# Latent attention: slots and rotary tables laid out anew, and another order of the filling work between the heads

## The chip, the cores and the metric

The kernel runs on one core of one Trainium2 chip. The metric is the device time of one execution in microseconds (us). Three runs of the kernel before took 1540.17, 1544.18 and 1545.57 us; the median is 1544.18 us. The profile is of one more execution.

The engines in this text are PE (TensorE: matrix products and transposes), DVE (VectorE: additions, products, reductions on tiles), ACT (ScalarE: casts, exponentials, square roots), POOL (GpSimd) and SP (SyncE), which here mostly issue transfers (DMAs).

## The reference

The model is a trunk of two layers on 528 positions: 16 learned meta tokens and 512 frames, each a vector of 1024 floats. Layer 0 mixes with retention, layer 1 with latent attention; each is followed by a gated feed-forward network (FFN) of hidden width 2816. Only layer 1's attention is touched by the change:

```
kv_a  = rmsnorm(h) @ w_kv_a                   # latent of 512, rotary key of 64
k, v  = rmsnorm(kv_a[:512]) @ w_kv_b          # 8 heads: 128 key, 128 value channels
cq    = rmsnorm(rmsnorm(h) @ w_q_a)           # 768
q     = cq @ w_q_b                            # 8 heads: 128 plain, 64 rotary channels
q_rot = [q1 * cos - q2 * sin, q1 * sin + q2 * cos]
for each block of 128 queries:
    sc = (q . k + q_rot . k_rot) * 192 ** -0.5, masked to earlier chunks of 64
    o  = softmax(sc) @ v
h = h + concat(o) @ w_o
h = h + (silu(n @ w1) * (n @ w3)) @ w2        # n = rmsnorm(h), the FFN behind it
```

## The kernel before

**Arithmetic.** Every product of two float32 tiles is made of three matmuls on tiles of a shorter float format: each operand is split into a high part `hi` and a low part `lo` (`split`, L320: ACT casts `hi`, DVE subtracts for `lo`), and `mm` (L358 and L360) adds hi x hi, hi x lo and lo x hi. The weights come by `weights` (L345): SP loads `raw`, ACT casts `whi`, DVE subtracts `wlo`, in a ring of three buffers each.

**Memory.** `slot()` (L279) takes a tile of 128 x 528 from the pool `sp` (45 slots in this stage) or from `yp`, eight slots at the right end of the memory. `temp()` takes one of the short-lived tiles `t`, `wide()` one of `e`. `acc` and `r` are constants of one slot's size, used for the norms; between the norm ahead of the attention and the FFN's norm both are idle. PSUM, where PE writes, holds four tiles `ps` of 1024 columns (`pp`); every product, every score block, every set of transposes takes one and gives it back when its last reader is done. A request for a tile waits until the one that has to be used again is free.

**The stage.** `mla` (L973) first makes the latent `ckv` and the query latent `cq`, and loads the rotary tables: `ktr` for the key, two tiles `qtr` for the queries. Then come two kinds of work, written out one behind the other in program order, which each engine follows.

*The heads* (loop from L1113). The 512 queries are four blocks. For head `n`, `scores(i)` makes block `i`'s scores with five products per stretch (L113), the maximum on DVE, the exponential on ACT (L124, tile `t`), and DVE scales the result (L126). `weights(i)` transposes that on PE (L139, L140) and splits it into `e` tiles; the 16 meta rows go to `meta_p` (L331). `values()` is twelve products (L156) and one with the meta rows (L157); its result is split into two slots and joins the list `att`. The loop runs a head behind: block 3's transposes and the values of head n-1 stand between the first scores of head n.

*The filling work.* `Filler` (L65) holds a dictionary of generators. `step()` takes the next step of the first one in the dictionary; `FILL[n]` (L56) says how many steps go into each of five gaps of head `n`. `until(name)` runs the first entries to their ends until `name` is gone; the loop calls `until(f"q{n}")` before head `n`. The generators are

- `query(n)`: one step, head n's queries (18 matmuls of L360 and a split).
- `rotary(g)`: the rotary channels of four heads; two products, then `rotate_queries` (L1171), where DVE multiplies with the tables and ACT and POOL's DMAs copy 32-row pieces into four heads' tiles (L1187).
- `keys_values(pr)`: seven steps for a pair of heads: two key products (L358, 24 rows of two matmuls), four value tiles and, as the fifth, the meta tokens' (`mla_values`, L1156; matmuls at L620).
- `project(pairs, g)`: four steps, each a product of six matmuls with half of the output weights and the addition to the residual `h[m]`. While the pair's two heads are not both in `att`, a step of it is empty (L1076).

**The tail** (L1133 to L1141). Behind head 7's last values, `until("p2")` runs what is left of the first half of pair 2's projection, `project([3], 0)` makes the first half of pair 3's, and `project([2, 3], 1)` makes the second halves of both in one sum. Each of its steps with pair 3 also calls `prep_ffn` (L479): ACT scales `h[m]` to an FFN input, `square_add` (L387) adds its squares to `acc` on DVE, and for every second `m` `operands` (L758) makes seven sums and splits them to the tile `xp`. Then the FFN begins (L910): its weights come as `raw`, some of them summed (`raw <- raw`), split to `whi` and `wlo`, and products go to PSUM tiles `a` and `b` (L827). `start` (L933) sums the squares and takes the root (L930).

Of the kernel before, what the change touches and what calls it, by code (L numbers as in the profile page):

```python
# [12 lines left out]
F32R = mybir.dt.float32r  # L13
# [6 lines left out]
P = 128  # L20
D = 1024
KD = D // P
SEQ = 512
META = 16
T = SEQ + META
# [17 lines left out]
RING = 3  # L43
EW = 4 * HT
RET_SLOTS = 45
MLA_SLOTS = 45

PARTS = (3, 3, 2, 3)

# [10 lines left out]
def drain(steps):  # L60
    for _ in steps:
        pass
# [26 lines left out]
class Head:  # L89
# [57 lines left out]
    def values(self):  # L147
        k, nc = self.k, self.nc
        po = k.ps()
        c = slice(self.vi * P, (self.vi + 1) * P)  # L150
        for j in range(4):
            vh, vl = (u[:, c] for u in self.v[j])
            q0 = min(j, 2) * P
            ph, pl = (z[j // 2][:, j % 2, q0:] for z in (self.ph, self.pl))
            for t, (x, y) in enumerate(((vh, ph), (vh, pl), (vl, ph))):
                nc.tensor.matmul(po[:, q0:SEQ], x, y, start=j == 0 and t == 0, stop=False)  # L156
        nc.tensor.matmul(po[:, :SEQ], self.v[4][:, c], self.pm[:, :SEQ], start=False, stop=True)  # L157
        pool = k.yp if self.n >= 2 else None
# [89 lines left out]
class Kernel:  # L248
# [724 lines left out]
    def mla(self):  # L973
        nc, a = self.nc, self.a
# [7 lines left out]
        r = self.r  # L982
        ktr = self.slot()
        nc.gpsimd.dma_start(out=ktr, in_=a["ktrig"])
        qtr = [self.slot(), self.slot()]
        for i in range(2):
            nc.gpsimd.dma_start(out=qtr[i][:, :SEQ], in_=a["qtrig"][:, i])
        self.ident = self.const([P, P], name="ident", src=a["ident"])
        self.ma = self.const([P, P], BF16, name="ma")
        nc.vector.memset(self.ma, 0.0)  # L990
# [40 lines left out]
            nc.gpsimd.dma_start(out=z[ROPE:P], in_=z[0:ROPE])  # L1031
        for _ in steps:
            next(norm, None)
        drain(norm)
        self.meta_tiles(ckv)

# [4 lines left out]
        def keys_values(pr):  # L1041

            kn = []
            whi, wlo = self.weights(a["w_kbk"][pr])
            for i in range(2):
                ps = self.ps()
                for k in range(4):
                    c = slice((i * 4 + k) * P, (i * 4 + k + 1) * P)
                    self.mm(ps, (whi[:, c], wlo[:, c]), ckv[k], k == 0, k == 3, True)
                hi, lo = (self.slot(F32R, None if pr else self.yp) for _ in range(2))  # L1050
# [46 lines left out]
        for i, _ in enumerate(norm):  # L1097
            if i % 2:
# [4 lines left out]
        drain(query(1))  # L1103


        order = {"q2": query(2), "q3": query(3), "r1": rotary(1), "q5": query(5), "p0": project([0], 0),
                 "p0b": project([0], 1), "kv2": keys_values(2), "q4": query(4), "kv3": keys_values(3), "q6": query(6),
                 "q7": query(7), "p1": project([1], 0), "p1b": project([1], 1), "p2": project([2], 0)}
        filler = Filler(order)
        prev = None  # L1110
        for n in range(MH):
# [21 lines left out]
        prev.weights(3)  # L1133
        filler.step()
        att.append(prev.values())
        filler.until("p2")
# [4 lines left out]
        drain(project([2, 3], 1))  # L1141

    def normed(self, raw, acc, name, n, full, out):
        w = T if full else SEQ
# [11 lines left out]
    def mla_values(self, pr, ckv, out):  # L1156

        w = self.weights(self.a["w_kbv"][pr])
        w = [[u[:, k * 256 : (k + 1) * 256] for u in w] for k in range(4)]
        pool = None if pr else self.yp  # L1160
        v = [(self.slot(F32R, pool), self.slot(F32R, pool)) for _ in range(2)]
        for j in range(5):
            if j < 4:
                c = (j % 2) * 256
                out.append([u[:, c : c + 256] for u in v[j // 2]])
            else:
                out.append(self.meta_v[pr // 2][:, pr % 2 * 256 : (pr % 2 + 1) * 256])
            self.token_rows(ckv, self.xm, w, j, out[j])
            yield

    def rotate_queries(self, got, tr, heads):  # L1171

        p1, p2 = got
        c, s = (z[:, :SEQ] for z in tr)
        parts = []
        for u, w, op in ((c, s, ALU.subtract), (s, c, ALU.add)):
            m1, m2 = self.slot()[:, :SEQ], self.slot()[:, :SEQ]
            self.tt(m1, p1, u, ALU.mult)
            self.tt(m2, p2, w, ALU.mult)
            parts.append((m1, m2, op))  # L1180
        for half, (m1, m2, op) in enumerate(parts):
            self.tt(m1, m1, m2, op)
            hi, lo = (self.slot(F32R)[:, :SEQ] for _ in range(2))
# [101 lines left out]
```

## Time and profile before

| | |
|---|---|
| runs | 1540.17, 1544.18, 1545.57 us (median 1544.18) |
| profiled execution | 1546.48 us; its span 1544.5 us |
| PE busy | 1442.9 us, 93% of the span |
| DVE busy | 1170.7 us, 76% |
| ACT busy | 768.0 us, 50% |
| POOL busy | 152.3 us, 10% |
| chain that ended last | PE 31%, DVE 8%, ACT 3%, DMA 1% of the span |
| DMA | 183.87 MB, mean 119 GB/s |

The span runs from the first to the last instruction in the trace; the execution's own time is 2.0 us longer. Times below are counted from the span's start. PE is the busy engine of the whole, but its share is a mean over stages. The latent attention lies between about 840 and 1165 us of the span; its heads run from about 960 to 1130 us, its tail from there on. In a timeline, a row is a run of like instructions: its start, its length, engine, line, operation, tiles, shape, count, and in brackets the idle time of the engine ahead of it with what ended that.

### The profile page before, as it was taken

The numbers are of one execution on the slowest core, as the hardware profiler recorded it, in microseconds if no ns is written. First come the engines' busy times: TensorE is split into PE (matmuls) and PEld (weight loads), VectorE is DVE, ScalarE is ACT, GpSimd is POOL, SyncE is SP. The second block draws the span as 40 slices with busy tenths as digits, with TensorE's granted clock in tenths as the row PEclk, the third lists the DMA queues.
The fourth block names the chain that finished last, engine by engine and source line by source line (L and its number), as shares of the span: only waits on it lengthen the run. The fifth ranks groups of instructions, "written<-read, shape, count | busy, mean of one in ns | idle before, by whom it ended". The sixth has DMA issues, their size and how long they took to land. (4 is left out here: it accounts for less than half of the span.)

```text
span 1544.5 us, 27868 instructions
## 1 busy us (share of the span) xinstructions
PE 1442.9 (93%) x10988; PEld 1388.2 (90%) x10988; DVE 1170.7 (76%) x1901; ACT 768.0 (50%) x1365; POOL 152.3 (10%) x196
## 2 busy tenths in 40 slices
PE   8999999999996999999988999899978999999984
PEld 8999999999996999989988988688858999989974
DVE  7675485484597998978988677676786988979886
ACT  5452342352465555545556446545465555545542
POOL 2000000000000111111121001000001111111120
PEclk9999999999998999999999999899988999999997
DMA  6222222122143667677656223201225776677562
GB/s 216 79 69 83 79 71 95 55 83 83 56 109 89 171 159 196 162 171 174 164 134 167 82 83 100 75 28 66 55 62 137 175 180 167 161 185 180 140 151 70
DMA packets 84803, 183.87 MB, mean 119 GB/s; under 512 B 9777, under 2 KB 30385, under 8 KB 84673
## 3 DMA queue, kind: packets, MB, share of 16 engines
q1 hardware_dynamic: 60336, 141.13, 29.3%
q0 software_dynamic: 24336, 40.98, 15.6%
q8 instruction: 86, 1.41, 0.4%
q14 instruction: 45, 0.36, 0.1%
HBM read 178.65 MB, written 2.10 MB: 117 GB/s over the span
## 5 line engine op out<-in xcount | busy, mean ns | idle before, releaser
L827 PE MATMUL b<-xp,whi 128*128 128x264 f32 (+1 forms) x2640 | 493.7, 287 | 23.2 <-ACT t L883 10.7
L322 ACT CAST whi<-raw 128x1024 fp32r<-128x1024 f32 (+5 forms) x428 | 364.2, 855 | 299.8 <-PE ps L358 152.1
L318 DVE TENSOR_TENSOR wlo<-raw,whi 128x1024 fp32r<-128x1024 f32 (+5 forms) x428 | 413.8, 977 | 61.2 <-ACT whi L322 59.1
L827 PEld LDWEIGHTS b<-xp,whi 128*128 128x128 f32 x2640 | 414.9, 192 | 26.7 <-ACT t L883 11.9
L827 PE MATMUL b<-xp,wlo 128*128 128x264 f32 (+1 forms) x1320 | 376.6, 285 | 0.0
L358 PE MATMUL ps<-s,whi 128*128 128x264 f32 x1824 | 303.2, 288 | 11.1 <-ACT whi L322 6.5
L358 PEld LDWEIGHTS ps<-s,whi 128*128 128x128 f32 x1824 | 256.9, 191 | 13.4 <-ACT whi L322 6.5
L827 PEld LDWEIGHTS b<-xp,wlo 128*128 128x128 f32 x1320 | 253.0, 192 | 0.0
L827 PE MATMUL a<-xp,whi 128*128 128x264 f32 (+1 forms) x1056 | 204.4, 289 | 5.0 <-ACT whi L322 5.0
L358 PE MATMUL ps<-s,wlo 128*128 128x264 f32 x912 | 187.2, 287 | 0.0
L827 PE MATMUL a<-xp,wlo 128*128 128x264 f32 (+1 forms) x528 | 156.3, 296 | 22.7 <-DVE wlo L318 21.9
L827 PEld LDWEIGHTS a<-xp,whi 128*128 128x128 f32 x1056 | 168.2, 194 | 5.7 <-ACT whi L322 5.6
L358 PEld LDWEIGHTS ps<-s,wlo 128*128 128x128 f32 x912 | 143.3, 191 | 0.1
L799 POOL DMA_DIRECT2D raw<-w x76 | 65.9, 867 | 774.5 <-DMA raw<-w 368.5
L827 PEld LDWEIGHTS a<-xp,wlo 128*128 128x128 f32 x528 | 102.9, 195 | 29.0 <-DVE wlo L318 28.7
L360 PE MATMUL ps<-s,whi 128*128 128x512 f32 x368 | 120.0, 407 | 4.3 <-ACT t L124 3.5
L620 PE MATMUL ps<-whi,s 128*128 128x256 f32 x640 | 115.4, 281 | 0.0
L318 DVE TENSOR_TENSOR s<-ps,s 128x256 fp32r<-128x256 f32 (+4 forms) x96 | 51.7, 557 | 71.2 <-ACT s L322 49.1
L620 PEld LDWEIGHTS ps<-whi,s 128*128 128x128 f32 x640 | 98.9, 188 | 0.2
L802 POOL DMA_DIRECT2D raw<-w x76 | 65.6, 863 | 250.2 <-DMA raw<-w 102.0
L620 PE MATMUL ps<-wlo,s 128*128 128x256 f32 x320 | 89.5, 280 | 0.0
L360 PEld LDWEIGHTS ps<-s,whi 128*128 128x128 f32 x368 | 68.8, 193 | 20.6 <-ACT t L124 4.1
(158 smaller groups left out, 1811.0 us busy)
## 6 DMA issues: line engine op xcount, KB each, us to landing
raw<-w SPq DMA_DIRECT2D x140, 256.0 KB, 3.8
raw<-w SPq DMA_DIRECT2D x44, 512.0 KB, 4.9
raw<-w POOLq DMA_DIRECT2D x88, 256.0 KB, 5.2
raw<-w SPq DMA_DIRECT2D x72, 192.0 KB, 3.1
raw<-w SPq DMA_DIRECT2D x24, 384.0 KB, 3.6
raw<-w POOLq DMA_DIRECT2D x48, 192.0 KB, 4.3
raw<-w_v SPq DMA_DIRECT2D x16, 512.0 KB, 3.8
raw<-w_g SPq DMA_DIRECT2D x16, 512.0 KB, 3.5
```

What stands on the lines that cost most here:

```text
L318: self.nc.vector.tensor_tensor(out=out, in0=a, in1=b, op=op)
L322: self.nc.scalar.copy(out=hi, in_=src)
L358: mm(ps[:, h * 512 : h * 512 + HT], w[p], x[q][:, h * HT : (h + 1) * HT], start=s, stop=e)
L360: mm(ps[:, :SEQ], w[p], x[q], start=s, stop=e)
L620: mm(ps[:, :256], x[k][p][:, c], w[k][q], start=k == 0 and i == 0, stop=k == last and i == 2)
L799: nc.gpsimd.dma_start(out=q.r1[:, 1], in_=q.part(3), accum_op=ALU.add)
L802: nc.gpsimd.dma_start(out=q.r3[:, 0], in_=q.part(0), accum_op=ALU.add)
L827: nc.tensor.matmul(bank, wt[u][:, cs], xp[:, p, v, :w], start=first and k == 0 and i == 0, stop=False, skip_group_check=True)
```

## The change

It has three parts, all in layer 1's attention.

- **Slots.** The two rotary tables of the queries go to `acc` and `r` and are loaded later, behind the query latent and behind the DMAs that copy the rotary key. In `rotate_queries` one of two products and the high part become temporaries, and the last subtraction or addition is written in the first loop. `sp` has 47 slots. `yp` serves the keys and values of pairs 0 and 2 (before: pair 0 alone) and the outputs of heads 6 and 7 (before: of heads 2 to 7).
- **Order.** In the filling table `q4` and `kv2` now stand ahead of pair 0's projection, `q5` behind it.
- **The second half of pair 2's projection** is an entry of its own (`p2b`), ended before the tail; the tail's last call has pair 3 alone.

```
--- before.py
+++ after.py
@@ -43,7 +43,7 @@
 RING = 3
 EW = 4 * HT
 RET_SLOTS = 45
-MLA_SLOTS = 45
+MLA_SLOTS = 47
 
 PARTS = (3, 3, 2, 3)
 
@@ -155,7 +155,7 @@
             for t, (x, y) in enumerate(((vh, ph), (vh, pl), (vl, ph))):
                 nc.tensor.matmul(po[:, q0:SEQ], x, y, start=j == 0 and t == 0, stop=False)
         nc.tensor.matmul(po[:, :SEQ], self.v[4][:, c], self.pm[:, :SEQ], start=False, stop=True)
-        pool = k.yp if self.n >= 2 else None
+        pool = k.yp if self.n >= 6 else None
         hi, lo = k.slot(F32R, pool), k.slot(F32R, pool)
         k.split(hi[:, :SEQ], lo[:, :SEQ], po[:, :SEQ])
         return hi, lo
@@ -982,9 +982,7 @@
         r = self.r
         ktr = self.slot()
         nc.gpsimd.dma_start(out=ktr, in_=a["ktrig"])
-        qtr = [self.slot(), self.slot()]
-        for i in range(2):
-            nc.gpsimd.dma_start(out=qtr[i][:, :SEQ], in_=a["qtrig"][:, i])
+        qtr = [self.acc, r]
         self.ident = self.const([P, P], name="ident", src=a["ident"])
         self.ma = self.const([P, P], BF16, name="ma")
         nc.vector.memset(self.ma, 0.0)
@@ -1031,6 +1029,8 @@
             nc.gpsimd.dma_start(out=z[ROPE:P], in_=z[0:ROPE])
         for _ in steps:
             next(norm, None)
+        for i in range(2):
+            nc.gpsimd.dma_start(out=qtr[i][:, :SEQ], in_=a["qtrig"][:, i])
         drain(norm)
         self.meta_tiles(ckv)
 
@@ -1047,7 +1047,7 @@
                 for k in range(4):
                     c = slice((i * 4 + k) * P, (i * 4 + k + 1) * P)
                     self.mm(ps, (whi[:, c], wlo[:, c]), ckv[k], k == 0, k == 3, True)
-                hi, lo = (self.slot(F32R, None if pr else self.yp) for _ in range(2))
+                hi, lo = (self.slot(F32R, None if pr % 2 else self.yp) for _ in range(2))
                 self.split(self.two(hi), self.two(lo), self.halves(ps))
                 kn.append((hi, lo))
                 yield
@@ -1103,9 +1103,7 @@
         drain(query(1))
 
 
-        order = {"q2": query(2), "q3": query(3), "r1": rotary(1), "q5": query(5), "p0": project([0], 0),
...
+        order = {"q2": query(2), "q3": query(3), "r1": rotary(1), "q4": query(4), "kv2": keys_values(2), "p0": project([0], 0), "p0b": project([0], 1), "q5": query(5), "q6": query(6), "kv3": keys_values(3), "q7": query(7), "p1": project([1], 0), "p1b": project([1], 1), "p2": project([2], 0), "p2b": project([2], 1)}
         filler = Filler(order)
         prev = None
         for n in range(MH):
@@ -1133,12 +1131,12 @@
         prev.weights(3)
         filler.step()
         att.append(prev.values())
-        filler.until("p2")
+        filler.until("p2b")
         self.shut("sp", "mm")
         self.wx = self.pool("wx")
         self.xp = self.pool("xp", bufs=4)
         drain(project([3], 0))
-        drain(project([2, 3], 1))
+        drain(project([3], 1))
 
     def normed(self, raw, acc, name, n, full, out):
         w = T if full else SEQ
@@ -1157,7 +1155,7 @@
 
         w = self.weights(self.a["w_kbv"][pr])
         w = [[u[:, k * 256 : (k + 1) * 256] for u in w] for k in range(4)]
-        pool = None if pr else self.yp
+        pool = None if pr % 2 else self.yp
         v = [(self.slot(F32R, pool), self.slot(F32R, pool)) for _ in range(2)]
         for j in range(5):
             if j < 4:
@@ -1174,13 +1172,14 @@
         c, s = (z[:, :SEQ] for z in tr)
         parts = []
         for u, w, op in ((c, s, ALU.subtract), (s, c, ALU.add)):
-            m1, m2 = self.slot()[:, :SEQ], self.slot()[:, :SEQ]
+            m1, m2 = self.slot()[:, :SEQ], self.temp()[:, :SEQ]
             self.tt(m1, p1, u, ALU.mult)
             self.tt(m2, p2, w, ALU.mult)
-            parts.append((m1, m2, op))
-        for half, (m1, m2, op) in enumerate(parts):
             self.tt(m1, m1, m2, op)
-            hi, lo = (self.slot(F32R)[:, :SEQ] for _ in range(2))
+            parts.append(m1)
+        for half, m1 in enumerate(parts):
+            hi = self.tp.tile([P, T], F32R, tag="tmp", name=self.name("t"))[:, :SEQ]
+            lo = self.slot(F32R)[:, :SEQ]
             self.split(hi, lo, m1)
             for j in range(4):
                 to, of = half * 32, slice(32 * j, 32 * j + 32)
```

How the instructions move on three engines, at the places that the prediction speaks of:

PE, at the end of head 1: behind the scores of its fourth block stand the transposes of its second and third, then (`L113`, 128x256) head 2's first scores. `ps` are PSUM tiles, `t` the scaled softmax blocks. Before:

```order
L115 MATMUL ps_11300<-mb,ma 128x64
L139 MATMUL ps_11319<-ident,t_11218 128x128 x2
L140 MATMUL ps_11319<-ident,t_11218 16x128
L139 MATMUL ps_11328<-ident,t_11279 128x128 x3
L140 MATMUL ps_11328<-ident,t_11279 16x128
L113 MATMUL ps_11340<-s_10658,s_10995 128x256
```

and of the change, where the tile `whi`/`wlo` holds the key weights of pair 2:

```order
L358 MATMUL ps_11361<-s_10406,wlo_11254 128x264 x2
L358 MATMUL ps_11361<-s_10447,whi_11253 128x264 x2
L358 MATMUL ps_11361<-s_10448,whi_11253 128x264 x2
L358 MATMUL ps_11361<-s_10447,wlo_11254 128x264 x2
L139 MATMUL ps_11390<-ident,t_11312 128x128 x3
L140 MATMUL ps_11390<-ident,t_11312 16x128
L113 MATMUL ps_11402<-s_10656,s_10993 128x256
L113 MATMUL ps_11402<-s_10657,s_10993 128x256
```

The transposes of the second block (`x2`) and of the third (`x3`) stood next to each other before; now the second key product of pair 2 (24 rows, of which the last four are seen) stands between them. The first key product stands in the gap ahead of head 0's values, where before had an empty step.

ACT, around the first exponential of head 1 (`L124`). `s` in the casts of `L322` is the high part of a rotary half, the casts of `L1187` (of the change `L1186`) copy its rows to the four heads, `ps` of 128x128 is a transposed block of head 0. Before:

```order
L322 CAST s_11147<-s_11138 128x512
L322 CAST e_11043<-ps_11159 128x128
L1187 CAST s_11134<-s_11138 32x512
L1187 CAST s_11135<-s_11138 32x512
L1187 CAST s_11136<-s_11138 32x512
L329 CAST meta_p_1251_9782<-ps_11159 16x128
L124 ACTIVATE t_11178,mx_11179<-ps_11171,mx_11179 128x144
```

and of the change:

```order
L322 CAST t_11146<-s_11136 128x512
L1186 CAST s_11132<-s_11136 32x512
L1186 CAST s_11133<-s_11136 32x512
L1186 CAST s_11134<-s_11136 32x512
L1186 CAST s_11135<-s_11136 32x512
L322 CAST e_11041<-ps_11158 128x128
L124 ACTIVATE t_11177,mx_11178<-ps_11170,mx_11178 128x144
```

Before, three of the four copies of the first half stand ahead of the exponential; now all four do, and the first of them stand ahead of the cast of head 0's block.

DVE, at the end of the attention. `h_64` to `h_71` are the eight residual tiles, the first to be added to in the tail is `h_64`; `s` is the low part of head 7's output. Before:

```order
L318 TENSOR_TENSOR meta_p_1252_9783<-ps_12677,meta_p_1252_9783 16x128
L318 TENSOR_TENSOR raw_1830_12922<-raw_12924 128x512
L318 TENSOR_TENSOR s_12705<-ps_12690,s_12704 128x512
L318 TENSOR_TENSOR h_64<-ps_12722,h_64 128x512
L318 TENSOR_TENSOR h_65<-ps_12733,h_65 128x512
L318 TENSOR_TENSOR e_12746<-e_12730 128x256
L318 TENSOR_TENSOR h_66<-ps_12757,h_66 128x512
L318 TENSOR_TENSOR e_12746<-e_12730,e_12746 128x256
```

and of the change, from the first addition behind head 7's last transposed block on:

```order
L318 TENSOR_TENSOR h_68<-ps_12712,h_68 128x512
L318 TENSOR_TENSOR s_12703<-ps_12688,s_12702 128x512
L318 TENSOR_TENSOR h_69<-ps_12720,h_69 128x512
L318 TENSOR_TENSOR h_70<-ps_12728,h_70 128x512
L318 TENSOR_TENSOR h_71<-ps_12736,h_71 128x512
L318 TENSOR_TENSOR raw_1832_12928<-raw_12930 128x512
L318 TENSOR_TENSOR wlo_12944<-raw_12926,whi_12943 128x1024
L318 TENSOR_TENSOR h_64<-ps_12758,h_64 128x512
L318 TENSOR_TENSOR h_65<-ps_12769,h_65 128x512
```

Four additions of pair 2's second half (`h_68` to `h_71`) now stand ahead of the tail's first one, and so does the low part `wlo` of an FFN weight, which before stood behind the tail's operands.

## Rows read from the trace of the kernel before

**Rows 1.** `Windows` of core 0: busy us and instructions per engine, then clock, DMA.

```profile
960.00:1020.00 60.00, 50.69 (x260) 41.56 (x259) 36.88 (x96) 31.46 (x81) 3.89 (x8) 0.91 0.23 66
1020.00:1056.00 36.00, 34.42 (x235) 30.89 (x234) 24.37 (x61) 18.02 (x48) 0.00 (x0) 1.00 0.20 67
1056.00:1113.00 57.00, 55.55 (x354) 48.63 (x353) 42.13 (x111) 30.50 (x84) 0.93 (x1) 1.00 0.19 55
```

**Rows 2.** Timeline of PE, heads 0 to 2: start, length, line, tiles, count, idle.

```profile
980.92 0.84 PE L113 MATMUL ps<-s,s 128*128 128x256 f32 x5
...
986.56 1.22 PE L360 MATMUL ps<-s,whi 128*128 128x512 f32 x2 [2.92 <-ACT t L124]
...
998.60 1.48 PE L113 MATMUL ps<-s,s 128*128 128x264 f32 x10 [1.55 <-ACT t L124]
...
1003.13 0.90 PE L139 MATMUL ps<-ident,t 128*128 128x128 f32 x3 [2.65 <-ACT t L124]
...
1003.90 1.42 PE L113 MATMUL ps<-s,s 128*128 128x256 f32 x5
...
1007.27 0.90 PE L113 MATMUL ps<-s,s 128*128 128x272 f32 x5 [0.91 <-ACT meta_p L331]
```

**Rows 3.** Timeline of ACT in head 1, same columns.

```profile
983.96 1.89 ACT L1187 CAST s<-s 32x512 fp32r<-32x512 f32 x3
...
986.04 0.38 ACT L124 ACTIVATE t<-ps,mx 128x144 f32<-128x144 f32 x1
```

**Rows 4.** Groups by line and shape, 930 to 1131 us: busy us, mean ns.

```profile
L322 ACT CAST s<-ps 128x256 fp32r<-128x256 f32 x12 | 4.4, 373 | 4.4 <-PE ps L620 4.2
```

**Rows 5.** Timeline of DVE, last use of `r` and first rotary products.

```profile
916.38 0.69 DVE L318 TENSOR_TENSOR s<-ps,r 128x512 f32<-128x512 f32 x1 [2.29 <-PE ps L360]
...
945.75 1.89 DVE L318 TENSOR_TENSOR s<-ps,s 128x512 f32<-128x512 f32 x3 [2.52 <-PE ps L360]
```

**Rows 6.** Timeline of PE, end of head 7 and last projections.

```profile
1124.88 0.63 PE L139 MATMUL ps<-ident,t 128*128 128x128 f32 x4 [2.84 <-DVE t L126]
...
1126.08 0.79 PE L156 MATMUL ps<-e,s 128*128 128x512 f32 x1 [0.46 <-ACT e L322]
...
1127.53 2.51 PE L156 MATMUL ps<-e,s 128*128 128x512 f32 x11
...
1130.11 0.40 PE L360 MATMUL ps<-s,wlo 128*128 128x512 f32 x1
...
1130.81 0.39 PE L360 MATMUL ps<-s,wlo 128*128 128x512 f32 x1
```

**Rows 7.** Timeline of PE, first products of layer 1's FFN.

```profile
1151.79 0.63 PE L827 MATMUL a<-xp,whi 128*128 128x256 f32 x2
1155.85 0.58 PE L827 MATMUL a<-xp,wlo 128*128 128x256 f32 x1 [3.44 <-DVE wlo L318]
1156.23 0.63 PE L827 MATMUL a<-xp,whi 128*128 128x256 f32 x2
```

**Rows 8.** Timeline of DVE, from the last values to the first FFN product.

```profile
1130.31 0.69 DVE L318 TENSOR_TENSOR raw<-raw 128x512 f32<-128x512 f32 x1 [2.35 <-PE ps L157]
1130.93 0.69 DVE L318 TENSOR_TENSOR s<-ps,s 128x512 fp32r<-128x512 f32 x1
1132.44 1.29 DVE L318 TENSOR_TENSOR h<-ps,h 128x512 f32<-128x512 f32 x2 [0.82 <-PE ps L360]
...
1152.64 1.02 DVE L318 TENSOR_TENSOR xp<-e,xp 128x512 fp32r<-128x512 f32 x2
...
1154.58 2.35 DVE L318 TENSOR_TENSOR wlo<-raw,whi 128x1024 fp32r<-128x1024 f32 x2
```

**Rows 9.** Timeline of ACT in the same stretch.

```profile
1154.69 1.04 ACT L322 CAST xp<-e 128x1024 fp32r<-128x1024 f32 x1 [1.96 <-DVE e L318]
1158.39 0.36 ACT L860 COPY b<-a 128x256 f32<-128x256 f32 x1 [2.65 <-PE a L827]
...
1161.34 0.47 ACT L930 ACTIVATE r<-a,eps_rms 128x256 f32<-128x256 f32 x1 [0.33 <-PE a L929]
```

More of the change, by code (lines that the diff above doesn't have):

```diff
@@ L157, in values @@
         nc.tensor.matmul(po[:, :SEQ], self.v[4][:, c], self.pm[:, :SEQ], start=False, stop=True)
-        pool = k.yp if self.n >= 2 else None
+        pool = k.yp if self.n >= 6 else None
         hi, lo = k.slot(F32R, pool), k.slot(F32R, pool)
@@ L984, in mla @@
         nc.gpsimd.dma_start(out=ktr, in_=a["ktrig"])
-        qtr = [self.slot(), self.slot()]
-        for i in range(2):
-            nc.gpsimd.dma_start(out=qtr[i][:, :SEQ], in_=a["qtrig"][:, i])
+        qtr = [self.acc, r]
         self.ident = self.const([P, P], name="ident", src=a["ident"])
@@ L1033, in mla @@
             next(norm, None)
+        for i in range(2):
+            nc.gpsimd.dma_start(out=qtr[i][:, :SEQ], in_=a["qtrig"][:, i])
         drain(norm)
@@ L1049, in keys_values @@
                     self.mm(ps, (whi[:, c], wlo[:, c]), ckv[k], k == 0, k == 3, True)
-                hi, lo = (self.slot(F32R, None if pr else self.yp) for _ in range(2))
+                hi, lo = (self.slot(F32R, None if pr % 2 else self.yp) for _ in range(2))
                 self.split(self.two(hi), self.two(lo), self.halves(ps))
@@ L1103, in mla @@
         drain(query(1))
-        order = {"q2": query(2), "q3": query(3), "r1": rotary(1), "q5": query(5), "p0": project([0], 0),
-                 "p0b": project([0], 1), "kv2": keys_values(2), "q4": query(4), "kv3": keys_values(3), "q6": query(6),
-                 "q7": query(7), "p1": project([1], 0), "p1b": project([1], 1), "p2": project([2], 0)}
+        order = {"q2": query(2), "q3": query(3), "r1": rotary(1), "q4": query(4), "kv2": keys_values(2), "p0": project([0], 0), "p0b": project([0], 1), "q5": query(5), "q6": query(6), "kv3": keys_values(3), "q7": query(7), "p1": project([1], 0), "p1b": project([1], 1), "p2": project([2], 0), "p2b": project([2], 1)}
         filler = Filler(order)
@@ L1135, in mla @@
         att.append(prev.values())
-        filler.until("p2")
+        filler.until("p2b")
         self.shut("sp", "mm")
@@ L1159, in mla_values @@
         w = [[u[:, k * 256 : (k + 1) * 256] for u in w] for k in range(4)]
-        pool = None if pr else self.yp
+        pool = None if pr % 2 else self.yp
         v = [(self.slot(F32R, pool), self.slot(F32R, pool)) for _ in range(2)]
@@ L1176, in rotate_queries @@
         for u, w, op in ((c, s, ALU.subtract), (s, c, ALU.add)):
-            m1, m2 = self.slot()[:, :SEQ], self.slot()[:, :SEQ]
+            m1, m2 = self.slot()[:, :SEQ], self.temp()[:, :SEQ]
             self.tt(m1, p1, u, ALU.mult)
             self.tt(m2, p2, w, ALU.mult)
-            parts.append((m1, m2, op))
-        for half, (m1, m2, op) in enumerate(parts):
             self.tt(m1, m1, m2, op)
-            hi, lo = (self.slot(F32R)[:, :SEQ] for _ in range(2))
+            parts.append(m1)
+        for half, m1 in enumerate(parts):
+            hi = self.tp.tile([P, T], F32R, tag="tmp", name=self.name("t"))[:, :SEQ]
+            lo = self.slot(F32R)[:, :SEQ]
             self.split(hi, lo, m1)
```

4 lines of the change are left out of this document (2 added, 2 removed).

## Prediction

> **What bounds the kernel now.** I first read the busy time by stretches of the attention stage, because the change touches nothing else. From 960 to 1020 us PE, the matmul engine, is busy 50.69 of 60 us, at a granted clock of 0.91; from 1020 to 1056 it is busy 34.42 of 36 us and from 1056 to 1113 it is busy 55.55 of 57 us, both at clock 1.00 [rows 1]. DVE and ACT are busy for about 60% and 50% of each stretch. So PE sets the time here, and what it loses is waiting, most of it in heads 0 to 2.
>
> Next I read PE's own timeline there, to see what ends each wait. The large ones are 2.92, 1.55 and 2.65 us, all ended by the exponential of a softmax (`ACT t L124`), and 0.91 us ended by the meta rows of the weights [rows 2]. A row that waits on the exponential is a matmul that wants a PSUM tile: there are four, and the exponential frees the one with the scores. After the first and the third wait the same work runs slower: five score matmuls take 1.42 us at 1003.90 and 0.84 us at 980.92. [...]
>
> Then the end of the stage. After the last scores PE waits 2.84 and 0.46 us for the softmax and the transposed weights of head 7 [rows 6], since no filling work is left. From 1132.44 on DVE is the bound: it works through the residual additions, squares and FFN operands until 1156.9 nearly without a pause [rows 8], and PE, done with the projections, starts the FFN's first product at 1151.79 and waits 3.44 us in the middle of it for a weight's low part [rows 7].
>
> **The new slots and tables.** The rotary tables go to `acc` and `r`. The last query pass reads `r` at 916.38 and the first rotary products start at 945.75 [rows 5], so about 29 us hide the later DMA; the rotary-key DMAs stand ahead of it on POOL's queue and nothing urgent behind it. Cost 0; uncovered it would be the landing time of one DMA. Fewer temporaries free slots, and no instruction in PE's way waits for those. The reordered rotary code puts four copies instead of three before head 1's first exponential on ACT. Three copies take 1.89 us [rows 3], so one is about 0.6 us; DVE brings the first half no later than before. The first wait of 2.92 us therefore stays and grows by **0.5 us** (bounds: 0, and 2.5 for four copies more).
>
> **The filling order, heads 1 to 3.** Up to that wait the work on PE is the same in both. Behind it, before has one query product (q5) and then nothing: `p0` comes next and gives an empty step while two heads' values are missing. After has a query product there too (q4), then both key products of pair 2, its five value tiles, and from the last step of head 2 on `p0`. PE's sum of work does not change; it is only placed where PE waited. So the gain is idle time that goes. From 987 to 1020 the idle time is 9.31 less 3.2 (the 2.92 and small ones before it), 6.1 us; with 1.58 and 1.45 of the next two stretches 9.1 us [rows 1, 2]. In the stretch from 1056 to 1113 each step of before does real work and PE idles 1.45 of 57 us, 2.5%. If all 126 us from 987 to 1113 become like that, 3.2 us remain and **5.9 us** go. Bounds: 0, if the waits come back elsewhere, and 9.1. I take 5.9, since the row nearest to the new order is that filled stretch. The low clock behind the 2.65 us wait goes as well: 0.58 us on the five scores and about as much on the transposes around them [rows 2], **1.2 us** (0 to 1.4). The low clock behind the 2.92 us wait stays.
>
> One wait is new. Pair 2's values go into the eight right-hand slots, and these hold pair 0's values until head 1 has read them. Three value tiles thus stay in three of the four PSUM tiles until head 1's value product is half through. Behind the waiting cast on ACT stand the next two casts, the head's output and the next exponentials. The first cast is released by the sixth of thirteen matmuls; the cast takes 0.37 us [rows 4] and the subtraction about as long, while PE still has seven matmuls, about 1 us. I charge **0.2 us**; below nothing it cannot be. The upper bound is a rival below.
>
> Together 5.9 + 1.2 - 0.5 - 0.2 = **6.4 us**.
>
> **The end of head 7.** After has three steps of pair 2's projection (18 matmuls) behind the last scores, which before has run by then. From 1130.11 to 1130.81 three such matmuls take 0.70 us [rows 6], so 18 are 4.2 us, and they cover the 2.84 and the 0.46 us. The low clock goes too: 1126.08 to 1127.53 holds three matmuls, 1.45 us instead of 0.70, and the eleven after them start slow [rows 6]; I count 1.0. Against it, DVE has the residual addition of such a step queued ahead of the softmax's last scaling, so that scaling waits for the step: 0.7 us. Sum 2.84 + 0.46 + 1.0 - 0.7 = **3.6 us** (0 to 4.3).
>
> **The tail.** The second half of pair 2's projection, 24 matmuls, leaves the DVE-bound tail, where it was hidden, and now stands ahead of it. Before, the last value product ends at 1130.3 and the first addition of the tail starts at 1132.44, 2.1 us later [rows 8]. After, five of the 24 come before that point and 19 follow: 19 x 0.233 = 4.4 us; then DVE does the last of their additions (0.65), a weight sum (0.65) and the low part of the FFN's first weight (1.2), in this order: 6.9 us. Loss 4.8 us. But that low part is one of the two that took 2.35 us from 1154.58 [rows 8] and held PE to 1155.85 [rows 7]. With it ready, nine of the twelve matmuls of the first product run early, and only three wait for the last operand. Before, the product ends at 1158.39 [rows 9], 25.95 us after 1132.44. After, the last operand comes at 1153.66 - 1132.44 = 21.2 us plus 0.35 for one more subtraction ahead of it, and three matmuls and the handover take 0.75: 22.3 us. Gain 3.65. Last, ACT now casts the last four operand blocks (1.04 us) ahead of the square root, which had 0.33 us to spare [rows 9]: loss 0.6. So the tail costs 4.8 - 3.65 + 0.6 = **1.75 us** (0.5 to 5.4). Behind it the FFN runs as before. The four additions of residuals that the split adds lie on DVE beside PE's 19 matmuls, 0.65 us each against 1.4 us a group.
>
> **Sum.** 6.4 + 3.6 - 1.75 = 8.2 us. The profiled execution took 1546.48 us (span 1544.5), so its like would take 1538.3; the median of the runs is 2.3 us lower, 1544.18, which gives **1536.0 us**, -0.53%.
>
> **Rivals.** *PSUM stays the limit.* The three large waits are for a PSUM tile, and each filling product wants one as well and adds a cast and a subtraction. Then heads 1 to 3 keep their waits, the 6.4 us are lost, and 3.6 - 1.75 remains: 1542.3. For it: what ends the waits [rows 2]. Against it: with the same four tiles the stretch from 1056 is filled to 97% [rows 1]. [...]
>
> *The tail shift is not repaid.* If the first FFN product still cannot start before the last operand, the tail costs 5.4 and the time is 1539.6. For it: PSUM must be handed over to the FFN before that product, after the last addition.
>
> *The held PSUM tiles jam head 2 (slower).* From the first held value tile to its release five tiles are taken by head 1's transposes and values and head 2's scores and transposes. If each waits as long as the mean of the three exponential waits, 2.37 us [rows 2], that is 11.9, and 1.2 for the low clock: 1536.0 + 13.1 = 1549.1. It decides from 8.2 us on, 1.6 us a tile. Against it: the release in the middle of the value product.
>
> *The first wait closes as well.* If the exponential comes earlier after all, 2.92 and some of the low clock behind it go: about 1531.
>
> **Chances.** Forecast (1532 to 1540) 0.56, PSUM limit 0.17, tail not repaid 0.14, jam 0.06, first wait closed 0.07. About 0.3%, 4.6 us, is what a measurement of this kernel can tell from no change: faster means below 1539.5. That is nearly all of the forecast, half of the second rival and the last: 0.67. Slower, above 1548.8, is the jam and a little unforeseen: 0.07; the rest 0.26. The range 1531 to 1544 leaves out the jam and the edges of the others.
>
> **What would show it.** PE's idle time between 987 and the last scores falls from 9.1 to about 3 us, with the clock at 1.00 from head 1's values on; the wait of about 3 us before q4 is still there. Head 2 shows no wait over 0.5 us behind head 1's value product. The last value product ends about 10 us earlier, around 1120; the first addition of the tail comes 7 us behind it, and no row of the first FFN product waits for `wlo`. I am wrong if PE idles 6 us or more in heads 1 to 3, or if the tail from the last value product to the root is over 4 us longer.

## The result, and the profile after

The changed kernel takes 1533.04 us (median of five runs, 1532.91 to 1535.3) against 1544.18: ratio 0.9931, 95% interval 0.9909 to 0.9953. It was timed twice more, each time beside other kernels on one chip: 0.9901 (0.9880 to 0.9922) and 0.9916 (0.9891 to 0.9941). The forecast was 1536.0 us, ratio 0.9947.

The profiled execution took 1532.99 us, its span is 1531.2 us, 13.3 less than before. Not all of that is the change. The stage's first latent matmul starts at 844.66 us before and at 846.95 after, behind identical work; and the rest of layer 1's FFN, identical again, took anything from 343 to 352 us in the profiles of this study. So the stage is measured from that matmul to the third copy of an FFN product on ACT behind the root, in three parts. First the rows at the two ends, of before and of after:

```profile
844.66 0.51 PE L358 MATMUL ps<-s,whi 128*128 128x264 f32 x2 [0.76 <-ACT s L334]
```

```profile
846.95 0.51 PE L358 MATMUL ps<-s,whi 128*128 128x264 f32 x2 [0.77 <-ACT s L334]
```

```profile
1193.07 0.36 ACT L860 COPY b<-a 128x256 f32<-128x256 f32 x1 [0.96 <-PE a L827]
```

```profile
1184.18 0.36 ACT L860 COPY b<-a 128x256 f32<-128x256 f32 x1 [0.96 <-PE a L827]
```

1193.07 - 844.66 is 348.4 us, 1184.18 - 846.95 is 337.2: the stage gained 11.2 us. The middle part is the clean one. It begins with the query product behind head 1's wait and ends where head 7's value product starts, and PE runs the same 780 matmuls in it in both kernels, only in another order. PE's windows of that part (length, busy us with the count, granted clock, then DMA), before and after:

```profile
986.50:1126.00 139.50, 127.09 (x780) 0.96 0.19 55
```

```profile
988.20:1114.60 126.40, 122.86 (x780) 0.99 0.19 55
```

Of 139.5 us, 12.4 were idle; of 126.4 us, 3.5 are. The busy time fell as well, by 4.2 us, and the clock's mean rose from 0.96 to 0.99. The stretches that answer to [rows 1]:

```profile
961.40:1020.00 58.60, 53.84 (x332) 46.99 (x331) 37.52 (x97) 34.23 (x85) 3.90 (x8) 0.97 0.26 76
1020.00:1056.00 36.00, 35.03 (x205) 29.80 (x205) 28.64 (x80) 19.83 (x59) 0.00 (x0) 1.00 0.18 56
1056.00:1101.00 45.00, 44.73 (x303) 40.31 (x302) 33.58 (x90) 24.94 (x71) 0.93 (x1) 1.00 0.20 60
```

From 1020 us on PE idles 1.2 of 81 us. All of PE's waits of over 0.5 us from head 1 to the last values are these, with the last value product (timeline; [rows 2, 6] have the largest of before):

```profile
988.21 0.75 PE L360 MATMUL ps<-s,whi 128*128 128x512 f32 x2 [3.36 <-ACT t L124]
...
1010.02 0.90 PE L113 MATMUL ps<-s,s 128*128 128x272 f32 x5 [0.98 <-ACT t L124]
...
1024.03 0.86 PE L113 MATMUL ps<-s,s 128*128 128x256 f32 x5 [0.97 <-DVE h L318]
```

```profile
1112.69 0.63 PE L139 MATMUL ps<-ident,t 128*128 128x128 f32 x4 [0.89 <-DVE t L126]
...
1117.97 0.50 PE L157 MATMUL ps<-meta_p,meta_v 80*128 80x512 f32 x1
```

The tail, on DVE, ACT and PE ([rows 7 to 9] before):

```profile
1125.27 1.28 DVE L318 TENSOR_TENSOR h<-ps,h 128x512 f32<-128x512 f32 x2
...
1147.02 1.22 DVE L318 TENSOR_TENSOR wlo<-raw,whi 128x1024 fp32r<-128x1024 f32 x1
...
1149.09 1.22 DVE L318 TENSOR_TENSOR wlo<-raw,whi 128x1024 fp32r<-128x1024 f32 x1
1150.23 1.22 DVE L318 TENSOR_TENSOR xp<-e,xp 128x1024 fp32r<-128x1024 f32 x1
```

```profile
1143.45 0.63 PE L827 MATMUL a<-xp,whi 128*128 128x256 f32 x2
...
1149.71 0.58 PE L827 MATMUL b<-xp,whi 128*128 128x256 f32 x1 [0.95 <-ACT xp L322]
1151.50 0.58 PE L827 MATMUL b<-xp,whi 128*128 128x256 f32 x1 [1.21 <-DVE xp L318]
```

```profile
1147.02 0.36 ACT L860 COPY b<-a 128x256 f32<-128x256 f32 x1 [1.24 <-PE a L827]
...
1153.19 0.47 ACT L930 ACTIVATE r<-a,eps_rms 128x256 f32<-128x256 f32 x1 [2.23 <-PE a L929]
```

The first product of the FFN runs from 1143.45 without a wait for a weight's low part, and its copy comes at 1147.02. But the second product now waits 0.95 us for the high part of the last operand and 1.21 us for its low part, which DVE makes at 1150.23, behind two low parts of weights and two sums; the root follows at 1153.19, 6.2 us after the copy. Before it followed 2.95 us after it [rows 9].

The stage of every kernel, in us, from the same landmarks (A: to head 1's query product; B: the 780 matmuls; C: from head 7's value product to the third copy), and its time against before on the same chip:

| kernel | A | B | C | stage | ratio (95%) |
|---|---|---|---|---|---|
| before | 141.9 | 139.5 | 67.0 | 348.4 | 1 |
| after | 141.3 | 126.4 | 69.5 | 337.2 | 0.9931 (0.9909 to 0.9953) |
| after, second | 141.2 | 124.9 | 70.7 | 336.8 | 0.9901 (0.9880 to 0.9922) |
| after, third | 141.2 | 126.3 | 70.7 | 338.2 | 0.9916 (0.9891 to 0.9941) |
| layout only | 141.1 | 134.3 | 71.1 | 346.5 | 0.9966 (0.9945 to 0.9987) |
| before, 47 slots | 142.4 | 132.7 | 67.4 | 342.6 | 0.9968 (0.9952 to 0.9983) |
| before, split tail | 141.9 | 140.6 | 64.6 | 347.1 | 0.9989 (0.9973 to 1.0004) |
| after, merged tail | 141.2 | 126.4 | 68.2 | 335.8 | 0.9899 (0.9877 to 0.9921) |
| merged, `yp` for 4 to 7 | 141.2 | 126.5 | 65.9 | 333.6 | 0.9905 (0.9887 to 0.9923) |
| after, rotary by DMA | 140.4 | 125.1 | 70.7 | 336.1 | 0.9933 (0.9908 to 0.9959) |
| merged, `yp`, DMA | 140.4 | 126.5 | 66.0 | 332.9 | 0.9897 (0.9869 to 0.9924) |
| after, pair 2's values in `sp` | 141.2 | 128.8 | 69.7 | 339.6 | 0.9933 (0.9912 to 0.9953) |
| merged, `yp`, rotary first | 143.1 | 125.0 | 65.3 | 333.4 | 0.9894 (0.9868 to 0.9920) |
| the same by DMA | 142.3 | 124.9 | 65.9 | 333.1 | 0.9899 (0.9874 to 0.9924) |

(The split tail has 18 matmuls more in B, 798.) An interval is about 3 us to either side, so the times tell the changed kernel (in its second and third timing) from the layout alone, not from its own variants; the stage, of which each kernel has one profile and the change three, is exact to some 1.5 us, which is what those three differ by.

### The profile page after: what moved, and what is told of

Read it like the earlier page. It is cut to its first block, busy times and chain, and to the rows that moved or that the text cites. A ratio compares the mean times of both kernels' runs of the same rounds, so it can differ in the third digit from the quotient of the medians.

```text
span 1531.2 us, 27869 instructions
## 1 busy us (share of the span) xinstructions
PE 1438.6 (94%) x10988; PEld 1386.0 (91%) x10988; DVE 1172.0 (77%) x1905; ACT 767.1 (50%) x1365; POOL 152.5 (10%) x196
## 5 line engine op out<-in xcount | busy, mean ns | idle before, releaser
L322 ACT CAST whi<-raw 128x1024 fp32r<-128x1024 f32 (+5 forms) x428 | 364.3, 855 | 299.0 <-PE ps L358 148.3
L358 PE MATMUL ps<-s,whi 128*128 128x264 f32 x1824 | 302.9, 288 | 11.2 <-ACT whi L322 6.6
L827 PEld LDWEIGHTS a<-xp,wlo 128*128 128x128 f32 x528 | 102.1, 193 | 25.1 <-DVE wlo L318 24.7
L318 DVE TENSOR_TENSOR s<-ps,s 128x256 fp32r<-128x256 f32 (+3 forms) x88 | 46.6, 546 | 65.0 <-ACT s L322 50.8
```

The source lines that it names most:

```text
L318: self.nc.vector.tensor_tensor(out=out, in0=a, in1=b, op=op)
L322: self.nc.scalar.copy(out=hi, in_=src)
L358: mm(ps[:, h * 512 : h * 512 + HT], w[p], x[q][:, h * HT : (h + 1) * HT], start=s, stop=e)
L827: nc.tensor.matmul(bank, wt[u][:, cs], xp[:, p, v, :w], start=first and k == 0 and i == 0, stop=False, skip_group_check=True)
```

## Experiments

**The layout alone**: the change with before's filling table and tail.

```
+        order = {"q2": query(2), "q3": query(3), "r1": rotary(1), "q5": query(5), "p0": project([0], 0),
...
+        filler.until("p2")
+        drain(project([2, 3], 1))
```

> The change's slots, tables and rotary code, with the order of filling work and the tail of before. Theory 1 (the gain is the filling order): as before, 1544 us within 2; PE still has waits of about 1.5, 2.7 and 2.8 us behind the exponentials of heads 1 and 2 and at the end of head 7, and the first wait in head 1 is about 0.5 us longer than the 2.92 of before (3.4). Rival (the layout itself gives the gain, because tables in constants and fewer temporaries free tiles earlier): 1533 to 1537 us and shorter waits.

Neither theory is right. The time fell by 0.3%, and B by 5.2 us, with the filling order of before. The waits of heads 1 and 2 went from five to two, though nothing was put in their place:

```profile
983.63 0.74 PE L360 MATMUL ps<-s,whi 128*128 128x512 f32 x2 [3.36 <-ACT t L124]
...
996.02 0.52 PE L139 MATMUL ps<-ident,t 128*128 128x128 f32 x3 [1.38 <-DVE mx L123]
...
998.00 0.78 PE L139 MATMUL ps<-ident,t 128*128 128x128 f32 x4 [0.72 <-DVE t L126]
```

So a good part of what the forecast gave to the order came from slots. C grew by 4.1 us, with a tail written as before. Where the slots come in is seen on ACT in before's head 1 (timeline):

```profile
999.75 0.62 ACT L1187 CAST s<-s 32x512 fp32r<-32x512 f32 x1 [0.92 <-PE ps L113]
1000.39 0.62 ACT L322 CAST s<-s 128x512 fp32r<-128x512 f32 x1
1001.03 0.62 ACT L1187 CAST s<-s 32x512 fp32r<-32x512 f32 x1
1001.67 0.59 ACT L322 CAST s<-ps 128x512 fp32r<-128x512 f32 x1
1002.28 0.70 ACT L124 ACTIVATE t<-ps,mx 128x528 f32<-128x528 f32 x1
```

The copy at 999.75 writes the tile of the fourth head's rotary queries. It waited for `PE ps L113`, a score matmul that gives it no data; the reading is that no slot was free until that matmul had read its tile for the last time. Behind it on ACT's queue stand the cast of a high part, another copy, a cast out of PSUM (1001.67), the exponential of 1002.28 and a second such cast (1002.98). The two casts are those of q5 and of head 0's output. With the scores that the exponential reads they hold three PSUM tiles, and PE waits until 1003.13 for that exponential [rows 2]. In these rows ACT runs them in that order, and the exponential starts 2.5 us behind the copy that waited.

**Before with 47 slots.**

```
-MLA_SLOTS = 45
+MLA_SLOTS = 47
```

> The kernel before with one number changed: 47 slots in `sp` instead of 45. Theory 4 (formed on the run with the layout alone: in the kernel before, copies of head 1's rotary pieces wait on ACT for a slot, and the casts and exponentials queued behind them hold the PSUM tiles that PE waits for): the waits of 1.55, 2.65, 0.91 and 0.62 us in heads 1 and 2 shrink to some 2 us together, the 780 matmuls from head 1's query product to head 7's value product take about 134 us instead of 139.5, the tail stays as before, ratio about 0.9965. Rival (not the number of slots but the temporaries and the tables in constants gave the 5 us): 138 us or more and a ratio of 1.000 within 0.002.

Theory 4 holds. B is 132.7 us, 6.8 less than before, and the tail keeps its length; the ratio is 0.9968, for some 0.9965 expected. Of the 6.8, PE's idle time gave 3.6 (12.4 to 8.8) and its busy time 3.2 (127.1 to 123.9), at a mean clock of 0.99 instead of 0.96. The waits of 1.55, 2.65, 0.91, 0.62 and 0.38 us became these:

```profile
1002.58 0.52 PE L139 MATMUL ps<-ident,t 128*128 128x128 f32 x3 [1.38 <-DVE mx L123]
...
1004.51 0.63 PE L139 MATMUL ps<-ident,t 128*128 128x128 f32 x4 [0.66 <-DVE t L126]
...
1006.22 2.21 PE L156 MATMUL ps<-e,s 128*128 128x512 f32 x12 [0.30 <-ACT t L124]
```

The exponential that came at 1002.28, 15.7 us behind the query product of head 1, now starts 12.1 us behind it. The copies are done 9 us ahead of it, none of them waited, and the cast of head 0's output runs at 998.41:

```profile
998.41 0.59 ACT L322 CAST s<-ps 128x512 fp32r<-128x512 f32 x1 [0.87 <-PE ps L157]
...
1000.43 0.59 ACT L124 ACTIVATE t<-ps,mx 128x400 f32<-128x400 f32 x1 [0.54 <-DVE mx L123]
...
1002.53 0.70 ACT L124 ACTIVATE t<-ps,mx 128x528 f32<-128x528 f32 x1 [0.27 <-DVE mx L123]
```

**The merged tail**: the change without `p2b`.

```
-        filler.until("p2b")
+        filler.until("p2")
...
-        drain(project([3], 1))
+        drain(project([2, 3], 1))
```

> The changed kernel, but the second half of pair 2's projection goes back into the tail, summed with pair 3's. Theory 1 (the order in the heads gives the gain, the split costs some 3 us in the tail): PE's 780 matmuls from the query product behind head 1's first wait to head 7's value product take 126 us as in the change; from the last value product to the root of the norm some 31 us instead of 34.8; 1529 to 1531 us. Rival 2 (the split gives a good part of the gain): 1536 to 1544 us. Rival 3 (the split costs nothing): 1533 us within 1.

B is 126.4 us, as in the change, so the split has no part in that gain. C is 1.3 to 2.5 us shorter than with the split. The ratio, 0.9899, is at the low end of the three of the change (0.9901 to 0.9931). Rival 2 is out, between the other two the times don't decide; the stage of 335.8 us puts the cost of the split at 1 to 2.4 us, less than theory 1 said and little more than profiles of one kernel differ by.

**Before with the split tail.**

```
+                 ... "p2": project([2], 0), "p2b": project([2], 1)}
...
-        filler.until("p2")
+        filler.until("p2b")
...
-        drain(project([2, 3], 1))
+        drain(project([3], 1))
```

> The kernel before, with one edit: the second half of pair 2's projection is a filling entry of its own, ended before the tail. Theory 1: three of its steps cover the end of head 7 (2.84 + 0.46 us of waits and some 1.2 us of low clock), one step stays ahead of the tail and costs about 1 us; heads 1 to 3 keep their waits: 1540 us within 1.5. Rival 2 (the split gives the gain): 1533 to 1536 us. Rival (what the cover gains, the tail gives back): 1544 us within 1.

The stage gained 1.3 us, no more than profiles of one kernel differ by, and the time nothing that can be told from zero. B holds 18 matmuls more, 4.2 us, and is only 1.1 longer, so the end of head 7 is covered as said; C is 2.4 shorter, of which 1.5 is the value product, which takes 2.7 us instead of 4.2, at a clock of 1.00 instead of 0.66 and without the two projection matmuls that stood in it. Gain and price nearly cancel: a projection that was free in a DVE-bound tail fills a wait on PE and is then no longer free.

**Where the merged tail loses**: the merged tail with the outputs of heads 4 to 7 in `yp`.

```
-        pool = k.yp if self.n >= 6 else None
+        pool = k.yp if self.n >= 4 else None
```

> The changed kernel with the second half of pair 2's projection merged into the tail again, and the outputs of heads 4 and 5 in `yp` as well (heads 4 to 7 instead of 6 and 7). Theory 5 (with the outputs of heads 4 and 5 in `sp`, the first operand tiles of the FFN, which lie over the closed `sp`, wait until the merged tail has read them): the 780 matmuls take 126.4 us as in the change, and from head 7's value product to the root's reciprocal it is some 35.5 us instead of 40.8 in the change and 38.3 in the merged tail with `sp`: ratio 0.9895 against before. Rival (the later operands were the order's doing): 38 us again and 0.991.

The mechanism is there, its worth is half. With the outputs of heads 4 and 5 in `sp`, DVE's first split of an operand comes 20.1 us after head 7's value product starts, with all of them in `yp` 9.8 us (rows of DVE, the merged tail and this one; the value products start at 1117.29 and 1120.10):

```profile
1137.35 4.23 DVE L318 TENSOR_TENSOR xp<-e,xp 128x512 fp32r<-128x512 f32 x6
```

```profile
1129.93 1.02 DVE L318 TENSOR_TENSOR xp<-e,xp 128x512 fp32r<-128x512 f32 x2
```

In the layout alone, whose tail reads heads 4 and 5 from `sp` as well, it comes 21.5 us behind; that is a part of its C of 71.1, but not all, since the merged tail has the same layout and a C of 68.2. With `yp`, C fell by 2.3 us, not 2.8, and the root's reciprocal comes 37.0 us after the value product's start, not 35.5: DVE has the same work to do in either order. The stage is 333.6 us, 3 to 5 less than the change's; the ratio, 0.9905, does not show it.

**Rotary pieces by DMA**: in the change, `rotate_queries` for the second group.

```
-                self.nc.scalar.copy(out=heads[j][to : to + 32, :SEQ], in_=m1[of])
+                if late:
+                    self.nc.gpsimd.dma_start(out=heads[j][to : to + 32, :SEQ], in_=hi[of])
+                else:
+                    self.nc.scalar.copy(out=heads[j][to : to + 32, :SEQ], in_=m1[of])
```

> The changed kernel, but the second group's rotary pieces (high parts) go to their heads by 8 more DMAs on POOL's queue instead of 8 copies on ACT. Theory 1 (head 1's exponential is late because four copies of 0.62 us stand ahead of it on ACT): the first wait falls from 3.36 us to about 1 us and the low clock behind it goes: 1529 to 1530.5 us. Rival (the exponential waits for the maximum or the transposed blocks on DVE): the wait stays over 2.5 us and the time is 1533 us within 1. Rival (the DMAs collide or come late for head 4): slower, 1534 to 1536 us.

Closest to the first rival: the wait fell from 3.36 to 2.61 us, not to 1. The copies are 0.75 us of it. The rest I put down to DVE, where two products, both sums and a subtraction of the group stand ahead of the maximum (L122) and of the low parts that the meta rows wait for; the cast of those rows (L331) now ends PE's wait. Of this kernel, PE and DVE:

```profile
984.41 0.74 PE L360 MATMUL ps<-s,whi 128*128 128x512 f32 x2 [2.61 <-ACT meta_p L331]
```

```profile
979.51 0.69 DVE L318 TENSOR_TENSOR t<-ps,r 128x512 f32<-128x512 f32 x1 [1.26 <-PE ps L360]
980.12 0.68 DVE L318 TENSOR_TENSOR t<-ps,acc 128x512 f32<-128x512 f32 x1
980.71 1.28 DVE L318 TENSOR_TENSOR s<-s,t 128x512 f32<-128x512 f32 x2
...
982.25 0.68 DVE L318 TENSOR_TENSOR s<-s,t 128x512 fp32r<-128x512 f32 x1
...
983.05 0.30 DVE L122 TENSOR_REDUCE mx<-ps 128x1 f32<-128x144 f32 x1
```

**The merged tail, `yp` and DMA together.**

> As the run with the merged tail and heads 4 to 7 in `yp`, and the second group's rotary pieces by POOL's DMAs instead of copies on ACT. The DMAs gained 1.1 us from the stage's start to head 1's query product and 1.4 us behind it: with both edits some 2 us less than with the first alone, ratio 0.988. Rival (what the DMAs gain is lost to other waits): the same ratio as the run without them.

332.9 us in the stage, 0.7 less than without the DMAs, where 2 were expected; the ratio of 0.9897 is the same within its interval, as the rival said. The 1.4 us that were expected in B were the clock's and not the DMAs': over the 6 us behind the first wait the clock was 1.00 in the run with DMAs alone, 0.72 in this one and 0.72 in the change.

**The changed kernel again**, twice.

> The changed kernel once more, beside the others on one chip: ratio 0.993 within 0.002.

> The changed kernel beside the others on one chip: ratio 0.992 within 0.002; from the stage's first latent matmul to the FFN's third copy 337 us, as in both profiles so far (337.2, 336.8).

The first came out a little faster than expected, the second as expected. In the second profile B is 1.5 us shorter than in the others, at the same 3.36 us of waiting ahead of it: see the last section.

**Pair 2's values in `sp`**: the change with one line as before.

```
-        pool = None if pr % 2 else self.yp
+        pool = None if pr else self.yp
```

> The changed kernel, but pair 2's values take slots of `sp` instead of the right-hand ones that head 1 still reads. The prediction charged 0.2 us for the casts that wait there for head 1's value product, its rival 13 us. Prediction: ACT's wait of 2.28 us for that product goes, the 780 matmuls from head 1's query product to head 7's value product take 126.2 us instead of 126.4. Rival (the held PSUM tiles cost more): 124 us or less. Other rival (four slots more from `sp` starve something else): over 127 us.

ACT's wait for head 1's value product is gone, but B is 128.8 us. Two things happen. PE's wait of 0.98 us ahead of head 2's second scores is gone too (the first row here against 1010.02 in the change), and head 1's value product starts 24.7 us behind the query product of head 1 instead of 25.5. Then, with four slots more taken from `sp`, new waits stand in head 2, of 1.55 and 0.95 us:

```profile
1013.23 0.89 PE L113 MATMUL ps<-s,s 128*128 128x272 f32 x5
...
1022.15 0.39 PE L620 MATMUL ps<-whi,s 128*128 128x256 f32 x1 [1.55 <-ACT t L124]
...
1025.68 1.49 PE L113 MATMUL ps<-s,s 128*128 128x264 f32 x10 [0.95 <-DVE t L318]
```

The other rival has the time right. The tiles held for the values cost some 0.8 us, for the 0.2 of the prediction, and the waits that came with four slots less cost more than that.

**The second rotary group first**: on the merged tail with `yp`.

```
-... "q2": query(2), "q3": query(3), "r1": rotary(1), "q4": query(4), ...
+... "r1": rotary(1), "q2": query(2), "q3": query(3), "q4": query(4), ...
```

> As the run with the merged tail and heads 4 to 7 in `yp`, with the second rotary group as the first entry of the filling table. Theory 6 (the wait of 3.4 us in head 1 is the rotary group's: its six products and sums on DVE stand ahead of head 1's maximum, its copies on ACT ahead of the exponential): with the group a head earlier that wait is under 1 us, and of the 2 us of low clock behind it nothing is left; the stage takes 329 to 331 us instead of 333.6. Rival (the wait moves into head 0, whose gaps now hold copies in place of matmuls): 333 to 336 us.

> The last kernel with the rotary pieces of the second group by POOL's DMAs. Theory 6: some 1 us less than the last. Rival: the same, since in head 0 the exponential waits for DVE.

Theory 6 falls. The wait only moved, into the end of head 0, and is as long as it was (PE, without and with the DMAs):

```profile
980.32 0.52 PE L139 MATMUL ps<-ident,t 128*128 128x128 f32 x3 [3.37 <-DVE mx L123]
```

```profile
979.93 0.52 PE L139 MATMUL ps<-ident,t 128*128 128x128 f32 x3 [2.69 <-DVE mx L123]
```

Both waits are ended by a maximum on DVE, so the reading is that it is the group's work on DVE, wherever it stands, that holds one back. B is 1.5 us shorter, A 1.9 longer, and with the DMAs the stage is the same within 0.3 us. No kernel of the study is shown faster than the change by its time.

## Why the prediction was right, and where not

The time and the sign were right, and the sum was near: 8.2 us forecast for the stage, 11.2 measured (11.6 and 10.2 in the other two profiles). A good part of that is luck, since the slots, put at nothing, did much of what the sum gave to the order. By its terms, sorted into the three parts:

| part | forecast | measured |
|---|---|---|
| A: the wait ahead of q4, +0.5 | +0.5 | -0.6 |
| B: idle time, -5.9 - 2.6 + 0.2 | -8.3 | -8.9 |
| B: clock | -1.2 | -4.2 |
| C: value product at full clock, -1.0; tail, +1.75 | +0.75 | -0.4 + 2.9 = +2.5 |
| sum | -8.25 | -11.2 |

- *The first wait.* It is there and grew from 2.92 to 3.36 us, by 0.44, for 0.5 forecast. A is shorter nonetheless, since 1.1 us were won ahead of it. PE's wait of 0.42 us ahead of the last query product, where head 0 starts, is gone in the change, and so is one of 0.30 us in head 1. The forecast had no term for these rows of before:

```profile
955.38 0.73 PE L360 MATMUL ps<-s,whi 128*128 128x512 f32 x2 [0.42 <-DVE s L318]
...
982.10 0.66 PE L139 MATMUL ps<-ident,t 128*128 128x128 f32 x4 [0.30 <-DVE s L318]
```

- *Slots: the step that failed.* "Fewer temporaries free slots, and no instruction in PE's way waits for those." The 47-slot run shows the opposite: two slots are worth 6.8 us of B and 5.8 of the stage. The rows for it were there. The wait of 0.92 us at 999.75 is in the timeline of ACT, and the order of ACT shown above has three of the four copies ahead of head 1's exponential; with 47 slots all four stand there. I read the waits on the exponential one step back, to ACT, and not to what ACT's queue stood behind.
- *The order.* Its mechanism is right for what is left: from the layout alone to the merged tail with the new order B falls from 134.3 to 126.4 us, 7.8 us, of which the cover at the end of head 7 is a part. The sum came out because the idle time that slots would have removed is the same idle time that the order was credited with. The new order without the new slots was not tried, so what the order gives by itself stays open.
- *The clock.* 1.2 us were counted for the scores and transposes behind one wait. That the low clock goes with the wait was the author's assumption: before, the clock is 1.00 from 998.6 to 1000.4, behind the wait of 1.55 us. Behind that of 2.65 us the stretch from 1003.1 to 1006.1 runs at 0.50, and behind the first wait the clock is at 0.51 before and at 0.72 after, over six us:

```profile
986.50:992.50 6.00, 5.94 (x14) 0.51 0.42 101
1003.10:1006.10 3.00, 2.97 (x15) 0.50 0.43 85
```

```profile
988.20:994.20 6.00, 5.99 (x20) 0.72 0.57 135
1005.20:1008.20 3.00, 2.81 (x25) 1.00 0.00 0
```

  In work at full clock that is (1 - 0.51) x 6 - (1 - 0.72) x 6 = 1.3 us and 0.50 x 3 = 1.5 us. Of the 4.2 us, 2.8 are so accounted for; the rest has no row of its own here. But where the low clock stands differs between executions. The split tail on the kernel before has the same heads, slots and waits there; it shows 0.72 behind the first wait too, and 0.50 in head 1's value product, where before has 1.00 (windows of that run):

```profile
991.15:997.15 6.00, 5.95 (x19) 0.72 0.41 101
1011.40:1015.00 3.60, 3.60 (x14) 0.50 0.00 0
```

  Summed over the stretches of heads 1 and 2, in work at full clock, the low clock costs 4.7 us before (a mean of 0.88 from 986.5 to 1026), 5.1 with the split tail and 1.7 in the change. I put the saving of some 3 us down to the change, which removed the waits of 1.55 and 2.65 us, but not the fact that 1.3 of it shows at the first wait, which the change did not remove. The forecast counted 1.2.
- *The end of head 7.* 2.84 and 0.46 us became 0.89, for 0.7 forecast.
- *The held PSUM tiles.* ACT waits 2.3 us for head 1's value product; PE's waits in head 2 are 0.98 and 0.97 us, the second of them behind head 1's value product, where the prediction wanted none over 0.5. The run with `sp` has the first one gone and puts the held tiles at 0.8 us, for 0.2 forecast. The rival of 13 us is out.
- *The tail.* The last value product to the first addition: 6.9 forecast, 6.8 measured (1118.47 to 1125.27). The first addition to the copy: 22.3 forecast, 21.75 measured. The copy to the root: +0.6 forecast, +3.2 measured. The step stopped at the first FFN product; the second needs the last operand too. In both kernels DVE makes that one behind two low parts of weights, 4.4 us after the first product's last operand before and 4.7 after; the low parts that were done earlier only made room for the next two. Before, the row is

```profile
1156.85 1.22 DVE L318 TENSOR_TENSOR xp<-e,xp 128x1024 fp32r<-128x1024 f32 x1
```

  and the first product, itself late, hid it. FFN work behind the root gave back some 0.7 us. The value product takes 3.8 us instead of 4.2, not 3.2: its clock is 1.00 instead of 0.66, but five projection matmuls stand in it where two did, and the sum had no term for those. From the end of the last value product to the root the tail takes 34.7 us instead of 31.1, close to the 4 us more that the prediction had set as a sign of being wrong.
- *PSUM stays the limit*, the rival with the highest chance, was wrong as it was put, but nearer the cause than the forecast: the tiles were held by a queue that waited for a slot (0.92 us at 999.75). I had weighed only PSUM. The 47-slot run shows that the slots had a large part in it, 6.8 us of B.

## What to carry to other kernels

A wait on a busy engine's result is not explained until the instruction ahead of it on that engine's queue is: follow one step further, to what that one waited for, and ask whether it is a buffer; here the exponential that ended PE's wait of 2.65 us started 2.5 us behind a copy that had waited 0.92 us, by the reading above for a slot. Where a change gives buffers and reorders work, try the buffers alone first; one number gave 5.8 of the 11.2 us that this change gained in its stage. Filling that was moved here from the tail, where DVE is the bound, into PE's gap at the end of head 7 gained the gap and lost the cover, and the two nearly cancelled: in the kernel before, C became 2.4 us shorter and B 1.1 us longer.

## What the runs showed of the hardware

After the same idle time of 3.36 us PE's clock behaved differently in executions of one program: in the first profile of the changed kernel it was 0.72 over the next 6 us, in the third 0.73, in the second it stayed at 1.00:

```profile
984.40:990.40 6.00, 5.94 (x32) 1.00 0.56 136
```

That is 1.5 us of B, 124.9 instead of 126.4, with no change in the code. After a wait of 2.92 us the clock was 0.51 over six us in the kernel before; over six us from the same query product it was 0.72 in its variant with the split tail, which has the same heads. And stages with identical instructions started 10 us apart in the profiles of this study (842.5 to 852.4 us for the first latent matmul), so that a difference of spans, 13.3 us here, says less than one of stages.
